# w_ada's products in pairs over quarters of PSUM, columns by transposes, and both first gate weights measured over TensorE

## The chip, the cores and the metric

The kernel runs on one core of one Trainium2 chip. The metric is the time of one execution on the device in microseconds (us), as the median of several runs. Times inside one execution come from one profiled execution, counted from the start of its span.

## What is computed

One decoder layer over 2048 tokens of width 1024, in float32. Cut to what matters here:

```
mod = silu(c) @ w_ada + b_ada            # (1, 3*1024)
shift, scale, gate = split(mod, 3)
h = rms_norm(x, g_pre) * (1 + scale) + shift
proj = h @ w_in        # qa, ka, va, fa, za, qb, kb, vb, zb
oa = forgetting_attention(qa, ka, va, fa + b_fgate) * silu(za)
ob = sliding_window_attention(rope(qb), rope(kb), vb, sinks) * silu(zb)   # window 128, 8 heads, 2 kv heads
y = concat(oa, ob) @ w_out
out = x + gate * rms_norm(y, g_post)
```

## The kernel before, in words

TensorE (PE) multiplies float16 pairs: every operand is split into a high and a low half, and a product is three matmuls (high times high, high times low, low times high). So each weight slice of `w_in` (128 columns) is loaded, its largest absolute value found (`w_max` or a reduction), turned into a power-of-two scale (`w_scale`), and split (`w_high` on ScalarE, ACT; `w_low` in two parts on VectorE, DVE). A product of a slice with one of four chunks of 512 tokens takes eight units of three matmuls.

**First stage** (a hand-written order; every engine executes its instructions in the order in which the code records them). It computes the two first thirds of `mod`: half 1 of `w_ada` (scale) and half 0 (shift), each eight tiles `wa` of 128 x 1024, loaded by the SyncE queue (SP) into eight buffers that half 0 reuses after half 1. In before, six tiles of half 1 and four of half 0 go through PE with `silb` (silu(c) spread over 128 columns) as weights, so that every one of PSUM's 128 partitions holds the same row of `mod` (L471, L589); the others are summed on DVE (L478, L480) and added by a product with ones. `ada_col` (L490, L492) turns the row into columns: times the identity, then summed along the free axis. From both halves comes a bound on h and from it a common scale `pH`, then the columns `Gp` and `Shp`. Meanwhile four x tiles are squared on ACT (`squares`, L372), normalised (`root`, `normal`), transposed on PE into `px` (`turn`, L390), and scaled by `Gp`, `Shp` on ACT into float32 `hf` and partly the float16 high half (L396); DVE makes the missing high halves (L400) and the low half (L401) of `hT[0]`. The weights `kb`, `vb` are measured over TensorE: a column of maxima is transposed, reduced, and sent to all partitions by a product with ones.

**First chunks.** For each chunk `ci` of 512 tokens the units stand in a list: kb, vb, and for `ci` < 3 the gate slices zb0 and zb1. `fill` runs through the list and before a unit runs the events hung at its number; every second unit a `tick` lets evacuations proceed, in steps that `after(n, f)` counts. The transposes of the next chunk stand between the gate units. The three PSUM banks `bk` are taken in turn and freed by the evacuation. The rotary evacuation (`evac_rope`) of kb copies the product (`qf`, ACT L697), sends it with four SP transfers to exchanged partitions (`qs`), multiplies by the cosine on DVE (`qc`, which frees the bank), by the sine on GpSimd (POOL, L711), adds (DVE L712) and splits into `stb`.

zb0's maximum is taken in the first stage (L633) and spread over PE inside the list (`z_row` at unit 6, `z_all` at 10, both in `bk[2]`, which also takes the second half of vb's product). zb1 goes another way, that of all later weights: its maxima go to DRAM (`mx_d`, POOL L214) and come back spread over the partitions (`mxr`, POOL L219), a reduction (L230) and `w_scale` follow, then `w_high` (L245) and `w_low` (L251).

**Sliding windows.** 32 windows of 256 queries (`Pair`) are interleaved with the remaining products. Each window has four ticks; DVE and ACT take the softmax, PE the scores (L831), transposes (L864) and values (L883). In passing, the squares of `w_out` are summed: 32 tiles `wsq`, loaded by SP and squared on ACT (L1085) one window later. Then follow the forgetting attention and the output product, which the change leaves alone.

Of the kernel before, what the change touches and what calls it, by code (L numbers as in the profile page):

```python
# [18 lines left out]
P = 128  # L19
# [21 lines left out]
def hybrid_layer(  # L41
# [109 lines left out]
    mxs = const.tile([P, 3], F32, name="mxs")  # L151
# [7 lines left out]
    mz = const.tile([1, 1], F32, name="mz")  # L159
# [26 lines left out]
    def after(n, f):  # L186
        late.append([n, f])
# [10 lines left out]
    first = ("kb", "vb", "zb0")  # L198
# [187 lines left out]
    def turn(ci, k):  # L386
# [6 lines left out]

        def scaled():
            for dst in ([hi] if k % 2 == 0 else []) + [hf[:]]:
                A.activation(dst, px[:], AF.Identity, scale=Gp[:, k:k + 1], bias=Shp[:, k:k + 1])  # L396

        def split():
            if k % 2:
                V.tensor_copy(hi, hf[:])  # L400
            V.tensor_tensor(lo, hf[:], hi, op=ALU.subtract)  # L401
# [19 lines left out]
    with tc.manual_schedule():  # L421
        rows = st.tile([P, P], F32, name="rows")
        posi = st.tile([P, CH], I32, name="posi")
        ifr = st.tile([P, 1], F32, name="ifr")
        V.memset(rows[:], 0.0)
# [11 lines left out]
        for k in range(1):  # L437
            load_ada(1, k)

        for g in range(4):  # L440
            SP.dma_start(posi[32 * g:32 * g + 32, :], positions[0, g * CH:(g + 1) * CH].partition_broadcast(32))
        SP.dma_start(ifr[:], inv_freq)
        for k in range(1, KT):
# [17 lines left out]
        silb = st.tile([P, KT, P], F32, name="silb")  # L461
        V.tensor_copy(silb[:], sil[:].unsqueeze(2).broadcast_to([P, KT, P]))

# [3 lines left out]
        acc = [st.tile([P, D], F32, name=f"acc{n}") for n in range(2)]  # L467

        def ada_mm(half, lhsT, rows_, begin, end):
            for n in range(2):  # L470
                PE.matmul(pm[half][n][:], lhsT, rows_[:, n * CH:(n + 1) * CH], start=begin, stop=end)  # L471

        def ada_pe(half, k, begin=False, end=False):
            ada_mm(half, silb[:, k, :], wa[half, k], begin, end)

        def ada_dve(half, k, first_):
            if first_:
                V.tensor_scalar(acc[half][:], wa[half, k][:], sil[:, k:k + 1], None, op0=ALU.mult)  # L478
            else:
                V.scalar_tensor_tensor(acc[half][:], wa[half, k][:], sil[:, k:k + 1], acc[half][:],  # L480
                                       op0=ALU.mult, op1=ALU.add)

        def ada_sum(half, end):
            ada_mm(half, ones[:], acc[half], False, end)

        def ada_col(half, dst):

            for n in range(2):
                dg = acc[half][:, n * CH:(n + 1) * CH].rearrange("p (k n) -> p k n", k=4)
                V.tensor_tensor(dg, pm[half][n][:].rearrange("p (k n) -> p k n", k=4),  # L490
                                ident[:].unsqueeze(1).broadcast_to([P, 4, P]), op=ALU.mult)
                V.tensor_reduce(dst[:, 4 * n:4 * n + 4], dg, axis=AX.X, op=ALU.add)  # L492

# [55 lines left out]
        for k in (0, 1, 3, 4, 6, 7):  # L549
            ada_pe(1, k, k == 0)  # L550
        for k in (2, 5):
            ada_dve(1, k, k == 2)
        for k in range(3):
            load_ada(0, k)
        for t in range(4):
            load_x(t)
        for k in range(3, KT):
            load_ada(0, k)
# [3 lines left out]
        ada_sum(1, True)  # L562

        mx3 = st.tile([P, 2], F32, name="mx3")
        for n, key in enumerate(first[:2]):
            V.tensor_reduce(mx3[:, n:n + 1], wq[key][0][:], axis=AX.XY, op=ALU.max, apply_absolute_value=True)
        ada_pe(0, 0, True)
        ada_pe(0, 3)
        PE.transpose(bk[0][0:2, 0:P], mx3[:], ident[:])
        ada_pe(0, 5)  # L570
        ada_dve(0, 1, True)
        ada_dve(0, 2, False)
        squares(0)
        scl0 = col8("scl0")
        ada_col(1, scl0)
        root(0)
        normal(0)
        m3 = st.tile([2, 1], F32, name="m3")
        V.tensor_reduce(m3[:], bk[0][0:2, 0:P], axis=AX.X, op=ALU.max)
        dg3 = st.tile([2, 2], F32, name="dg3")  # L580
        V.tensor_scalar(dg3[:], ident[0:2, 0:2], m3[:], None, op0=ALU.mult)
        PE.matmul(bk[0][:, P:P + 2], ones[0:2, :], dg3[:], start=True, stop=True)
        ada_dve(0, 4, False)
        ada_dve(0, 6, False)

        for n in range(2):
            nn = slice(n * CH, (n + 1) * CH)
            PE.matmul(pm[0][n][:], ones[:], acc[0][:, nn], start=False, stop=False)
            PE.matmul(pm[0][n][:], silb[:, KT - 1, :], wa[0, KT - 1][:, nn], start=False, stop=True)  # L589
        V.tensor_copy(mxs[:, 0:2], bk[0][:, P:P + 2])  # L590
        for n, key in enumerate(first[:2]):
            wq[key].append(mxs[:, n:n + 1])
        w_scale("kb")
        w_high("kb")
        w_scale("vb")
        w_low("kb", 0, 1)
        scl1 = col8("scl1")
        V.tensor_tensor(scl1[:], scl0[:], cols[:, 24:32], op=ALU.add)
        gcol = col8("gcol")
        V.scalar_tensor_tensor(gcol[:], scl1[:], 1.0, cols[:, 8:16], op0=ALU.add, op1=ALU.mult)  # L600
        absg = col8("absg")
        V.scalar_tensor_tensor(absg[:], gcol[:], -1.0, gcol[:], op0=ALU.mult, op1=ALU.max)
        turned = [turn(0, k) for k in range(5)]
        squares(1)
        w_high("vb")
        shf0 = col8("shf0")
        ada_col(0, shf0)
        shf = col8("shf")
        V.tensor_tensor(shf[:], shf0[:], cols[:, 16:24], op=ALU.add)
        abss = col8("abss")  # L610
        V.scalar_tensor_tensor(abss[:], shf[:], -1.0, shf[:], op0=ALU.mult, op1=ALU.max)
        bnd = col8("bnd")
        V.scalar_tensor_tensor(bnd[:], absg[:], 32.0, abss[:], op0=ALU.mult, op1=ALU.add)
        bmx = st.tile([P, 1], F32, name="bmx")
        V.tensor_reduce(bmx[:], bnd[:], axis=AX.X, op=ALU.max)

        PE.transpose(bk[0][0:1, 0:P], bmx[:], ident[:])
        bm = st.tile([1, 1], F32, name="bm")
        V.tensor_reduce(bm[:], bk[0][0:1, 0:P], axis=AX.X, op=ALU.max)
        PE.matmul(bk[0][:, P:P + 1], ones[0:1, :], bm[:], start=True, stop=True)  # L620
        pow2_floor(pH[:], bk[0][:, P:P + 1], "p2t")
# [3 lines left out]
        V.tensor_scalar(Shp[:], shf[:], ipH[:], 2.0 ** 14, op0=ALU.mult, op1=ALU.mult)  # L625

        V.tensor_scalar(pfl[:], ipH[:], 0.5, None, op0=ALU.mult)
        w_low("vb", 0, 1)
        for k in range(KT):
            turned[k][0]()  # L630
            turned[k][1]()
            if k == 2:
                V.tensor_reduce(mxs[:, 2:3], wq["zb0"][0][:], axis=AX.XY, op=ALU.max, apply_absolute_value=True)  # L633
            if k + 5 < KT:
                turned.append(turn(0, k + 5))
        root(1)
        normal(1)
# [48 lines left out]

    def evac_rope(ci, finish, pool):
        cols_ = slice(ci * CH, (ci + 1) * CH)

        def evac(ps, free):  # L690
# [20 lines left out]
            after(5, lambda: G.tensor_tensor(qs[:], qs[:], sinT[:, cols_], op=ALU.mult))  # L711
            after(6, lambda: V.tensor_tensor(qc[:], qc[:], qs[:], op=ALU.add))  # L712
# [886 lines left out]
```

## Time and profile before

| | |
|---|---|
| median of 3 runs | 1227.26 us (1226.62 to 1228.86) |
| profiled execution, its own time | 1225.7 us |
| its span | 1223.5 us |
| PE busy | 1161.8 us, 95% of the span |
| DVE, ACT busy | 906.5 and 674.6 us |

The 2.2 us between the profiled execution's time and its span lie outside the instructions. A timeline row gives start, duration, engine, line, operation, output and inputs, and in brackets how long the engine had been idle and what ended that. Rows with the same line and operation are merged with a count. In PE's rows a float32 matmul stands as two passes. A row that ends in an issuing queue (SPq, POOLq) is the issue of a transfer, not the transfer.

### The profile page before, as it was taken

What the parts mean: (1) busy time and instruction counts of PE and PEld (TensorE: products, weight loads), DVE (VectorE), ACT (ScalarE), POOL (GpSimd) and SP (SyncE); (2) the same over time, 40 slices, a digit from 0 to 9 for tenths busy, and PEclk for the clock granted to TensorE, in tenths of its full rate; (3) what the DMA queues carried; (4) which work ended last, traced back from release to release, by engine and by line L of the source; (5) the groups of instructions that cost most, each with busy time, mean ns of one, the idle gap of its engine ahead of it and who ended that gap; (6) DMA issues with size and microseconds to landing.
All of it is one profiled execution on the core that took longest, in us unless ns stands there. A gap on an engine that the chain in (4) does not pass through costs nothing.

```text
span 1223.5 us, 27396 instructions
## 1 busy us (share of the span) xinstructions
PE 1161.8 (95%) x10832; PEld 694.4 (57%) x10832; DVE 906.5 (74%) x2268; ACT 674.6 (55%) x1117; POOL 141.4 (12%) x252
## 2 busy tenths in 40 slices
PE   6769999999999999999999999999999979999997
PEld 2446746755558985555555555555555546555553
DVE  6756656677877656788888799878978797676665
ACT  2665434555555461466666666666766788433231
POOL 2001122233323210101000110010000000000000
PEclk8879999999999999999999999999999999999999
DMA  9654432423423432223325322122111146446652
GB/s 322 204 123 130 115 76 64 69 77 94 90 64 89 65 56 57 73 57 92 66 75 73 92 66 71 42 64 55 41 40 45 45 130 190 134 158 195 191 172 84
DMA packets 88036, 120.71 MB, mean 99 GB/s; under 512 B 27836, under 2 KB 63716, under 8 KB 87908
## 3 DMA queue, kind: packets, MB, share of 16 engines
q1 hardware_dynamic: 76932, 85.94, 24.9%
q0 software_dynamic: 10976, 33.03, 11.7%
q8 instruction: 85, 1.39, 0.6%
q14 instruction: 43, 0.35, 0.1%
HBM read 71.56 MB, written 25.18 MB: 79 GB/s over the span
## 4 chain that ended last, share of the span: by engine, by line
PE 79%; DVE 9%; DMA 4%; issue 3%; SPq 2%; ACT 2%; POOL 1%; DVEq 0%; POOLq 0%; ACTq 0%
PE bk L307 31%; PE bk L1407 13%; PE bk L325 6%; PE sta L1258 4%; PE bk L1209 4%; PE sta L1259 4%; PE poa L1284 2%; PE poa L1285 2%; PE poa L1282 2%; PE pxb L864 2%; PE pss L831 2%; PE pob L883 2%; DVE pha L1272 2%; DVE a_m L1212 1%; PE bk L1370 1%
## 5 line engine op out<-in xcount | busy, mean ns | idle before, releaser
L1265 ACT ACTIVATE p<-sta,lift,scl_qk 128x1024 f32<-128x1024 f32 (+2 forms) x160 | 171.8, 1074 | 134.3 <-PE sta L1259 78.5
L307 PE MATMUL bk<-hT,wh_qk 128*128 128x512 f16 x768 | 194.7, 379 | 0.4 <-DVE a_m L1212 0.4
L1407 PE MATMUL bk<-wohl,oz 128*128 128x512 f16 x768 | 172.4, 379 | 1.8 <-ACT wohl L1347 0.8
L1272 DVE TENSOR_TENSOR pha<-p,pha 128x1024 f16<-128x1024 f32 (+2 forms) x160 | 169.2, 1057 | 0.0
L1212 DVE TENSOR_REDUCE a_m<-bk 128x1 f32<-128x512 f32 x192 | 130.3, 686 | 52.3 <-PE bk L1209 51.7
L1269 ACT ACTIVATE pha<-p 128x1024 f16<-128x1024 f32 (+2 forms) x160 | 148.0, 925 | 7.3 <-PE poa L1285 1.4
L1407 PEld LDWEIGHTS <-oz 128*128 128x128 f16 x768 | 74.4, 99 | 83.8 <-issue 1.8
L1282 PE MATMUL poa<-vt,pha 128*128 128x65 f16 x1088 | 116.9, 193 | 3.0 <-DVE ona L1291 3.0
L1285 PE MATMUL poa<-vt,pha 128*128 128x65 f16 x1088 | 116.7, 193 | 1.1 <-DVE pha L1272 1.1
L1284 PE MATMUL poa<-vt,pha 128*128 128x64 f16 x1088 | 117.0, 195 | 0.0
L1258 PE MATMUL sta<-T 128*128 128x512 f16 (+1 forms) x320 | 112.0, 350 | 4.7 <-ACT p L1265 4.6
L307 PEld LDWEIGHTS <-wh_qk 128*128 128x128 f16 x768 | 72.4, 97 | 75.2 <-issue 1.4
L1209 PE MATMUL bk<-T 66*128 66x512 f16 (+2 forms) x320 | 109.9, 350 | 2.8 <-DMA T<-stq 2.3
L1282 PEld LDWEIGHTS <-pha 128*128 128x128 f16 x1088 | 101.9, 97 | 17.8 <-DVE ona L1291 4.3
L1259 PE MATMUL sta<-T 69*128 69x512 f16 (+1 forms) x320 | 110.7, 351 | 0.0
L1284 PEld LDWEIGHTS <-pha 128*128 128x128 f16 x1088 | 101.2, 97 | 11.5 <-issue 0.3
L1285 PEld LDWEIGHTS <-pha 128*128 128x128 f16 x1088 | 101.2, 99 | 1.3 <-DVE pha L1272 1.3
L307 PE MATMUL bk<-hT,wh_zb 128*128 128x512 f16 x384 | 92.4, 386 | 9.8 <-ACT wh_zb L245 9.1
L307 PE MATMUL bk<-hT,wh_za 128*128 128x512 f16 x384 | 99.9, 379 | 0.0
L325 PE MATMUL bk<-wh_va,hT 128*128 128x128 f16 x1536 | 91.2, 220 | 0.0
L325 PEld LDWEIGHTS <-hT 128*128 128x128 f16 x1536 | 87.5, 98 | 5.4 <-issue 2.6
L307 PE MATMUL bk<-hT,wh_qb 128*128 128x512 f16 x384 | 87.4, 380 | 0.0
(491 smaller groups left out, 1880.1 us busy)
## 6 DMA issues: line engine op xcount, KB each, us to landing
wa<-in_w_ada_dram SPq DMA_DIRECT2D x16, 512.0 KB
z_d<-tz POOLq DMA_DIRECT2D x32, 256.0 KB, 2.9
T<-stq SPq DMA_DIRECT2D x128, 64.0 KB
T<-o_d SPq DMA_DIRECT2D x16, 512.0 KB
T<-z_d SPq DMA_DIRECT2D x16, 512.0 KB
xr<-in_x_dram SPq DMA_DIRECT2D x16, 512.0 KB
out_dram<-yg SPq DMA_DIRECT2D x15, 512.0 KB
xt<-in_x_dram SPq DMA_DIRECT2D x12, 512.0 KB
```

The lines of the kernel that those rows point to most:

```text
L307: PE.matmul(ps, whl[:, a, k, :], hT[ci][:, b, k, :], start=(k == 0 and n == 0), stop=(k == KT - 1 and n == 2))
L325: PE.matmul(ps[:, u * P:(u + 1) * P], hT[ci][:, a, k, u * P:(u + 1) * P], whl[:, b, k, :], start=(k == 0 and n == 0), stop=(k == KT - 1 an ...
L1209: PE.matmul(mx[:, :w], T[0:XM, 0, i * P:(i + 1) * P], T[0:XM, 2, pc * CH:pc * CH + w], start=True, stop=True)
L1258: PE.matmul(self.st[:, o:o + w], T[:, 3, kb_], T[:, 1, qc], start=True, stop=False)
L1259: PE.matmul(self.st[:, o:o + w], T[0:XR, 2, kb_], T[0:XR, 0, qc], start=False, stop=not diag)
L1265: A.activation(self.p32[:, :self.w], self.st[:, :self.w], AF.Exp, scale=scl[f"qk{self.hd}"][:], bias=lift[:])
L1269: A.activation(self.ph[:, 0, :self.w], self.p32[:, :self.w], AF.Copy)
L1272: V.tensor_tensor(self.ph[:, 1, :self.w], self.p32[:, :self.w], self.ph[:, 0, :self.w], op=ALU.subtract)
L1282: PE.matmul(po[:, u, :], ph[:, 0, pq], vt[:, b, hd, 0:65], start=(self.first and n == 0 and u == 0), stop=False)
L1284: PE.matmul(po[:, u, 0:64], ph[:, 0, pq], vt[:, b, hd, 65:VW], start=False, stop=False)
L1285: PE.matmul(po[:, u, :], ph[:, 1, pq], vt[:, b, hd, 0:65], start=False, stop=(self.last and n == len(self.blocks) - 1))
L1407: PE.matmul(py, self.hl[:, i, k, :], w_slot(8 * j + k)[:, cc], start=(k == 0 and m_ == 0), stop=(k == KT - 1 and m_ == 2))
```

## The change

- All sixteen tiles of `w_ada` go through PE, two at a time: `silb` has only 32 columns per tile, and tile k writes into quarter k mod 4 of PSUM's partitions (k and k+4 add up). Each half is then copied to SBUF (`ada_row`, ACT), transposed in 128-column blocks (`ada_turn`, PE), and the four quarters are summed by a reduction of 16 values per row (`ada_col`).
- The bound that leads to `pH` is taken apart: the part from half 1 and the biases (`pre`) is ready early; half 0 gives only the largest absolute value of its rows (`rm`, `rmx`), added over the quarters by a product with `sel`.
- `inv_freq` and the positions are loaded from ACT's queue; `zb0` is no longer loaded a second time by POOL; x tiles 0 to 3 are loaded before half 0; zb1 is loaded by SP in the first stage.
- zb0 and zb1 are both measured over PE (`z_row` at 8, `z_all` at 11). zb1's scale and split stand at units 18 to 25 of the list.
- For chunk 0, ACT makes the high half of tiles 0 and 4 only. `squares(1)` follows the whole of chunk 0's scaling; `root(1)` and `normal(1)` move into the list; the transposes of chunk 1 stand three units later.
- In the sliding windows the rotary evacuation's later steps come one tick later, and `wsq` has three buffers and is squared two windows after its load instead of one.

```diff
-    first = ("kb", "vb", "zb0")
+    first = ("kb", "vb", "zb0", "zb1")
...
+        high = k % 2 == 0 if ci else k in (0, 4)
...
+        A.dma_start(ifr[:], inv_freq)
+        for g in range(4):
+            A.dma_start(posi[32 * g:32 * g + 32, :], positions[0, g * CH:(g + 1) * CH].partition_broadcast(32))
...
-        for key in first:
+        for key in first[:2]:
             w_load(key, pieces(key))
...
-        silb = st.tile([P, KT, P], F32, name="silb")
+        silb = st.tile([P, KT, 32], F32, name="silb")
...
+        def ada_two(half, k):
             for n in range(2):
+                for k_ in (k, k + 1):
+                    q = slice(32 * (k_ % 4), 32 * (k_ % 4) + 32)
+                    PE.matmul(pm[half][n][q, :], silb[:, k_, :], wa[half, k_][:, n * CH:(n + 1) * CH],
+                              start=k_ < 4, stop=k_ >= 4)
+        def ada_row(half, n):
+            A.activation(arow[half][:, n * CH:(n + 1) * CH], pm[half][n][:], AF.Copy)
+        def ada_turn(half, n):
+            for k in range(4):
+                PE.transpose(pm[half][n][:, k * P:(k + 1) * P], arow[half][:, (4 * n + k) * P:(4 * n + k + 1) * P],
+                             ident[:])
+        def ada_col(half, n, dst):
+            V.tensor_reduce(dst[:, 4 * n:4 * n + 4],
+                            pm[half][n][:].rearrange("p (k q r) -> p k q r", k=4, q=4)[:, :, :, 0],
+                            axis=AX.X, op=ALU.add)
...
         for t in range(4):
             load_x(t)
-        for k in range(3, KT):
+        for k in range(KT):
             load_ada(0, k)
         w_load("zb0", pieces("zb0"), SP)
         for t in range(4, 8):
             load_x(t)
-        ada_sum(1, True)
+        w_load("zb1", pieces("zb1"), SP)
+        for k in range(0, KT, 2):
+            ada_two(1, k)
...
+        for k in range(0, KT, 2):
+            ada_two(0, k)
+        rm = st.tile([P, 2], F32, name="rm")
+        for n in range(2):
+            V.tensor_reduce(rm[:, n:n + 1], pm[0][n][:], axis=AX.X, op=ALU.max, apply_absolute_value=True)
+            ada_row(0, n)
...
+        turned = [turn(0, 0)]
+        ada_turn(0, 0)
+        turned.append(turn(0, 1))
+        PE.matmul(bk[0][:, P:P + 1], sel[:], rmx[:], start=True, stop=True)
+        ada_turn(0, 1)
+        turned += [turn(0, k) for k in (2, 3, 4)]
...
-        root(1)
-        normal(1)
+        V.tensor_reduce(mxs[:, 3:4], wq["zb1"][0][:], axis=AX.XY, op=ALU.max, apply_absolute_value=True)
+        squares(1)
...
-    at_slice(6, z_row)
-    at_slice(10, z_all)
+    at_slice(8, z_row)
+    at_slice(11, z_all)
+    at_slice(9, lambda: root(1))
+    for u in range(4):
+        at_slice(10 + u, lambda u=u: normal(1, (u,)))
...
+            d = turn_lag[0]
+            after(5 + d, lambda: G.tensor_tensor(qs[:], qs[:], sinT[:, cols_], op=ALU.mult))
...
-        wsp = swa_pool("wsp", 2)
+        wsp = swa_pool("wsp", 3)
```

How the order moves is shown at three places. The first is PE at half 0 of `w_ada`; before, `wa` tiles with 128 columns of weights, and sums of ones with `acc`, the part summed on DVE:

```order
L471 MATMUL bk_135<-wa_281,silb 128x512
L471 MATMUL bk_136<-wa_281,silb 128x512
L582 MATMUL bk_134<-dg_349,ones 128x2
L588 MATMUL bk_135<-acc_202,ones 128x512
L589 MATMUL bk_135<-wa_285,silb 128x512
L588 MATMUL bk_136<-acc_202,ones 128x512
L589 MATMUL bk_136<-wa_285,silb 128x512
L390 MATMUL px<-ident,xt_269 128x128
```

The same place on PE in the change, from the last pair of tiles on; 32x512 is the output, `bk_134` and `bk_135` are the two banks of half 0:

```order
L474 MATMUL bk_134<-wa_272,silb 32x512
L474 MATMUL bk_134<-wa_274,silb 32x512
L474 MATMUL bk_135<-wa_272,silb 32x512
L474 MATMUL bk_135<-wa_274,silb 32x512
L389 MATMUL px<-ident,xt_252 128x128
L389 MATMUL px<-ident,xt_254 128x128
L389 MATMUL px<-ident,xt_256 128x128
L389 MATMUL px<-ident,xt_258 128x128
L482 MATMUL bk_134<-ident,arow_205 128x128 x4
```

No matmul waits for a sum made on DVE any more; the transposes of x and of the row take the place of the sums. The second place is DVE behind chunk 0, in before: `w_mx` is zb1's reduction, whose way goes over DRAM, and `mxr` what comes back; `stb` is kb's rotary result.

```order
L752 SCALAR_TENSOR_TENSOR vb<-bk_136,vb 128x2x64 x2
L754 SCALAR_TENSOR_TENSOR fl<-bk_136,kf,bfg 128x16
L230 TENSOR_REDUCE w_mx_767<-mxr 128x1
L86 TENSOR_SCALAR w_p_770<-w_mx_767 128x1
L87 TENSOR_SCALAR w_pw<-w_p_770 128x1
L236 RECIPROCAL w_sw<-w_pw 128x1
L237 TENSOR_SCALAR w_sw<-w_sw 128x1
L706 TENSOR_TENSOR stb<-qc,stb 128x512
```

There, in the change, up to the point where the measured maxima leave PSUM (`bk_135`):

```order
L106 SCALAR_TENSOR_TENSOR rst<-rs_t,rs_y 128x4
L699 SCALAR_TENSOR_TENSOR qc<-bk_133,cosT 128x512
L383 TENSOR_SCALAR hT_107<-hT_107,rst 128x1024
L937 COPY mxs<-bk_135 128x2
L383 TENSOR_SCALAR hT_107<-hT_107,rst 128x1024
L86 TENSOR_SCALAR w_p_685<-mxs 128x1
```

The copy of the maxima now stands behind the root of chunk 1, the cosine product and one normalisation; the reduction over `mxr` is gone for zb1. The third place is ACT after chunk 0, in the change; `wh_zb_798` is zb1's high half, `tz` a gate's tanh, `junk` a square of an x tile of chunk 2:

```order
L711 ACTIVATE stb<-qc 128x512
L397 ACTIVATE hT_105<-px,Shp,Gp 128x512
L397 ACTIVATE hf<-px,Shp,Gp 128x512
L244 ACTIVATE wh_zb_798<-wr_zb_282,w_sw 128x1024
L397 ACTIVATE hf<-px,Shp,Gp 128x512
L397 ACTIVATE hT_105<-px,Shp,Gp 128x512
L397 ACTIVATE hf<-px,Shp,Gp 128x512
L350 ACT_TABLE_LOAD
L350 ACTIVATE tz<-bk_133,cz_zb_766 128x512
L397 ACTIVATE hf<-px,Shp,Gp 128x512
L371 ACTIVATE junk,ss<-xt_699 128x1024
```

All of chunk 1's scaling now stands behind `stb`, that is behind the whole rotary evacuation of chunk 0's kb; before, its first tile stood ahead of it.

More of the change, by code (lines that the diff above doesn't have):

```diff
@@ L466, in hybrid_layer @@
         pm = {1: [ps_x.tile([P, CH], F32, tag="x", name="pm") for _ in range(2)], 0: [bk[1], bk[2]]}
[L467 to L469 removed]
+        arow = [st.tile([P, D], F32, name=f"arow{n}") for n in range(2)]
+        def ada_two(half, k):
             for n in range(2):
[L471 to L474 removed]
@@ L596, in hybrid_layer @@
+        normal(0)
         w_low("kb", 0, 1)
[L597 to L606, printed above, removed]
```

164 lines of the change are left out of this document (76 added, 88 removed).

## The prediction

> **What bounds the kernel now.** I read the waits of PE first, since PE is busy 1161.8 of 1223.5 us, the busiest engine; columns: engine and line, who ended the wait, total, times, longest.
>
> ```profile
> PE bk L307 <- ACT wh_zb L245: 9.1, 1, 9.1
> PE bk L307 <- ACT hT L396: 3.5, 1, 3.5
> PE pob L883 <- DVE ptb L869: 3.0, 2, 2.1
> PE pss L831 <- issue: 1.6, 1, 1.6
> ```
>
> The longest wait of all is one for zb1's high half. The busy times by stretch say where PE idles: columns are the stretch, its length, then busy time of PE, PEld, DVE, ACT, POOL, granted clock, DMA share, GB/s.
>
> ```profile
> 0.00:83.00 83.00, 54.14 (x256) 29.32 (x256) 54.48 (x142) 39.24 (x59) 10.41 (x21) 0.87 0.74 230
> 83.00:150.00 67.00, 66.29 (x510) 42.99 (x510) 41.86 (x102) 39.72 (x67) 8.80 (x12) 0.96 0.44 120
> 150.00:260.00 110.00, 105.08 (x1089) 69.51 (x1086) 69.63 (x209) 51.03 (x139) 27.28 (x49) 0.98 0.32 68
> ```
>
> 29 us are idle before 83 us, 0.7 in the next 67, 4.9 in the 110 after. From 83 us on PE sets the pace, so what is won before is kept. I therefore follow the first 98 us to one mark, the end of kb's product of chunk 1, and treat the windows apart. The timeline's rows on the way to it:
>
> ```profile
> 32.49 1.98 PE L471 MATMUL bk<-wa,silb 128*128 128x512 f32 x4 [2.63 <-DMA wa<-in_w_ada_dram]
> 35.05 1.99 PE L471 MATMUL bk<-wa,silb 128*128 128x512 f32 x4 [0.47 <-DMA wa<-in_w_ada_dram]
> 40.46 1.02 PE L589 MATMUL bk<-wa,silb 128*128 128x512 f32 x2
> 46.97 1.06 ACT L372 ACTIVATE junk<-hT 128x1024 bf16<-128x1024 f32 x1 [1.86 <-DMA hT<-in_x_dram]
> 49.93 0.59 PE L307 MATMUL bk<-hT,wh_kb 128*128 128x512 f16 x1 [3.50 <-ACT hT L396]
> 57.77 1.73 PE L307 MATMUL bk<-hT,wh_kb 128*128 128x512 f16 x6
> 65.87 0.81 PE L307 MATMUL bk<-hT,wh_zb 128*128 128x512 f16 x3
> 73.69 0.54 POOL L219 DMA_DIRECT2D mxr<-mx_d  x1 [7.85 <-DMA cosT<-cs__241]
> 79.80 0.29 DVE L230 TENSOR_REDUCE w_mx<-mxr 128x1 f32<-128x128 f32 x1 [2.41 <-DMA mxr<-mx_d]
> 82.08 1.03 PE L307 MATMUL bk<-hT,wh_zb 128*128 128x512 f16 x2 [9.12 <-ACT wh_zb L245]
> 92.39 5.34 PE L307 MATMUL bk<-hT,wh_kb 128*128 128x512 f16 x24
> ```
>
> Transfers bind until half 0 of w_ada has landed, then a chain over PE, DVE and ACT leads to the first kb product at 49.93; kb ends at 59.5 and zb0 starts at 65.87. zb1's way over DRAM (back at 79.80) holds PE until 82.08. The mark is at 97.7 (92.39 + 5.34).
>
> **Step 1, the last tile of w_ada lands.** Tiles 3 and 5 of half 0 end waits at 32.49 and 35.05: 1.28 us per tile, so tile 7 lands near 37.6. The bytes ahead of it stay the same, less POOL's extra load of zb0 (1024 x 128 numbers, a tile's size, so 1.28 us). The positions leave SP's queue, which should let the first tiles follow closer; I give that 0.8 us, between 0 and 3. Forecast 35.5 (33.5 to 36.3).
>
> **Step 2, its products.** Four matmuls follow its landing, eight passes. In a steady run each pass has one weight load like this:
>
> ```profile
> 27.98 0.19 PEld L471 LDWEIGHTS bk<-wa,silb 128*128 128x128 f32 x1 [0.24 <-issue]
> ```
>
> So a pass starts every 0.19 + 0.24 = 0.43 us. One after the other the eight take 3.44 us, fully overlapped in pairs 1.72. No run shows a matmul on a quarter of the columns; these are the two ends. I take 1.72, since neighbours in the order write different quarters: 37.2. The Trainium skill's page "TensorE: Matmul & The Clock Gate", Part 3, gives 2.38 times for three column tiles; by that, as an estimate 1.59 times for two, the eight would take 2.16 us and the sum be 0.4 us worse.
>
> **Step 3, from the last product to kb.** Before, 41.5 (40.46 + 1.02) to 49.93: 8.45 us, with masked sums on DVE, then ACT held by `squares(1)`, which waited for x until 46.97, and by wh_vb. Both leave this place. What is left, priced by these rows of the groups (mean ns behind the comma):
>
> ```profile
> L492 DVE TENSOR_REDUCE shf<-acc 128x4 f32<-128x512 f32 x2 | 1.4, 686 | 0.1
> L396 ACT ACTIVATE hf<-px,Shp,Gp 128x512 f32<-128x512 f32 x20 | 15.1, 780 | 0.3 <-PE px L390 0.3
> L401 DVE TENSOR_TENSOR hT<-hf,hT 128x512 f16<-128x512 f32 x20 | 13.3, 688 | 1.8 <-ACT hf L396 1.5
> L400 DVE CAST hT<-hf 128x512 f16<-128x512 f32 x10 | 4.2, 423 | 3.3 <-ACT hf L396 3.3
> L633 DVE TENSOR_REDUCE mxs<-wr_zb 128x1 f32<-128x1024 f32 x1 | 1.2, 1212 | 0.0
> L104 DVE TENSOR_TENSOR rs_t<-rs_t,rs_v 128x4 f32<-128x4 f32 x9 | 1.5, 162 | 0.3
> ```
>
> One reduction of a bank after the last product (0.7, the other overlaps), 0.3 of crossing, `rmx` 0.2; then sel's two passes, under 0.43 each, behind transposes of x and of the row, with the crossing to DVE 1.4; seven small DVE operations at 0.2 (0.16 and a gap) are 1.5; ACT's first scaling 0.8 and 0.1 to PE. Sum 5.0 (4 to 6). kb starts at 42.2, 7.7 us early.
>
> **Step 4, kb of chunk 0.** DVE binds: after the first `hf` (0.75) come 8 x 0.69 + 6 x 0.42 + 1.21 = 9.3, plus gaps 0.4; before, four casts only, 0.85 less. kb ends at 52.9 against 59.5: 6.6 early.
>
> **Step 5, to zb0.** The prices, beside the small operations above:
>
> ```profile
> L372 ACT ACTIVATE junk<-xt 128x1024 bf16<-128x1024 f32 x8 | 8.4, 1054 | 3.8 <-DMA xt<-in_x_dram 3.5
> L372 ACT ACTIVATION_READ_ACCUMULATOR junk<-xt 128x1 f32 x8 | 1.5, 189 | 0.0
> 61.16 3.72 PE L740 MATMUL bk<-wh_vb,hT 128*128 128x136 f16 x60
> ```
>
> The new waits: `z_row` on PE needs zb1's maximum, queued on DVE behind the whole loop, so all of vb's product stands 0.9 us, until 53.9. `squares(1)`, four times 1.25 on ACT behind the last scaling at 48.2, ends at 53.3. On DVE zb1's maximum and five small operations last to 54.9, the root of 13 operations at 0.17 to 57.2, then cosine and one normalisation, 0.7 each, and only then are the maxima copied out of `bk[2]` at 58.7. PE's second half of vb (48 matmuls at 0.062, 3.0 us) needs that bank; the first is done at 57.2 with the small products between: another 1.7 us idle. zb0's scale on DVE (a normalisation and four small operations later) is ready at 60.3, its high half on ACT at 61.4, hidden by vb, which ends at 62.0. zb0 starts at 62.1: only 3.8 us early.
>
> **Step 6, zb0 and zb1.** A tile's transposes and two units, in chunk 1:
>
> ```profile
> 104.33 0.60 PE L390 MATMUL px<-ident,xt 128*128 128x128 f32 x4
> 104.77 1.46 PE L307 MATMUL bk<-hT,wh_zb 128*128 128x512 f16 x6
> 106.07 0.60 PE L390 MATMUL px<-ident,xt 128*128 128x128 f32 x4
> ```
>
> From start to start 0.44 and 1.30 (0.22 a matmul): 48 matmuls are 10.4, eight tiles of transposes 3.5, together 13.9. The wait for DRAM is gone. What is late next is kb's rotary result, then zb1's high half:
>
> ```profile
> 103.50 1.27 POOL L711 TENSOR_TENSOR qs<-qs,sinT 128x512 f32<-128x512 f32 x1 [7.80 <-DMA qs<-qf]
> 98.43 3.53 SPq L699 DMA_DIRECT2D qs<-qf  x4
> L245 ACT ACTIVATE wh_zb<-wr_zb,w_sw 128x1024 f16<-128x1024 f32 x2 | 2.3, 1146 | 2.0 <-DVE w_sw L237 2.0
> 84.05 1.28 ACT L351 ACT_TABLE_LOAD   x1
> ```
>
> In chunk 1 the exchange takes 5.1 us from issue to POOL's multiply. From `qf` at 53.9 that gives 59.3; POOL is free by then. DVE's add stands behind zb0's low half (62.9), so `stb` runs on ACT at 64.1. Then two scalings, 66.2, and zb1's high half until 67.4. PE needs it at 69.0. zb1 hides; kb of chunk 1 may start at 76.0.
>
> **Step 7, kb of chunk 1.** From `stb` on, ACT has no gap: 12 scalings x 0.77, zb1's half 1.15, the table load 1.28, two tanh and `stb` at no more than a scaling, 2.1, four squares 5.0: 18.7 from 64.1, so the last `hf` ends at 82.7. Cast and subtraction on DVE, 1.2, and one unit, 0.65: the mark at 84.6. PE alone would reach it at 81.3, so ACT costs 3.3. Gain 97.7 - 84.6 = **13.1**. Chunks 1 and 2 stay PE's: ACT needs some 18 of 24.7 us there.
>
> **Step 8, the windows.** Between 150 and 260 us:
>
> ```profile
> DVE qc L712 <- POOL qs L711: 15.0, 5, 8.1
> ACT wsq L1085 <- DMA wsq<-in_w_out_dram: 5.5, 1, 5.5
> 215.56 0.69 DVE L706 TENSOR_TENSOR stb<-qc,stb 128x512 f16<-128x512 f32 x1
> 217.36 0.83 PE L831 MATMUL pss<-kst,stb 64*128 64x256 f16 x12
> 225.80 0.72 PE L831 MATMUL pss<-kst,stb 64*128 64x256 f16 x10
> ```
>
> The tick and the third buffer shorten waits by which DVE and ACT hand `ptb` late to PE (3.0). POOL's share, waiting for maxima from DRAM, stays. I take half, 1.5; bounds: all 4.6 with the issue gap, or 2.1 lost (one tick, a quarter of the window from 217.36 to 225.80). At the end two squares instead of one: 0.6 on ACT, partly seen, I take 0.3.
>
> **The sum.** 13.1 + 1.5 - 0.3 = 14.3. The profiled execution's 1225.7 (span 1223.5 and 2.2 around it) becomes 1211.4. It lies 1.6 under the median of 1227.26; the same saving gives **1213.0**.
>
> **The rivals.** First, the pairs don't overlap (20%). Half 0 is then 32 passes of 0.43, 13.8 us, started when its second tile is there (35.5 - 6 x 1.28 = 27.8): 41.6, not 37.2. All behind comes 4.4 later: 1217.4. For it: float32 passes that each fill the array's time; against: different quarters. The same page and Part 3 say that weight loads overlap running matmuls only when the row group differs, and here all 128 rows are used by both; by that rule this case happens, and no run here shows it.
>
> Second, faster (8%): the copy of step 5 and ACT's queue of step 7 cost nothing, because the early transfers run at full rate and the squares end sooner. 1.7 + 3.3 come back: 1208.0.
>
> Third, slower (6%): the later rotary steps reach the scores. A piece's `stb` is done at 215.56, its scores start at 225.80: 10.2 us slack, 9.5 beyond the row's own duration. A tick is 2.1. Only if POOL's and DVE's waits grow by over 7 us besides does each of the 14 pieces cost a tick: 29 less the gain of 13.1 and 0.3 more at the end, about 1243. Waits of 8.1 are in the table; but these are paid already.
>
> Fourth, no change (4%): a stall at zb0 or at kb of chunk 1 takes all 13.1 back, as when x of chunk 2 lands over 10 us after its square is due (72 us): 1227. Before, those loads were never waited for.
>
> **How the numbers follow.** The forecast has 62%. Its own range: step 1 (-2, +0.8), step 3 (1 either way), step 8 (-3, +3.7), rarely together: 1208 to 1217. With the first rival at the upper end and the second at the lower: 1207 to 1220. A measurement can tell about 0.2%, 2.5 us. Faster: 62 + 20 + 8 = 90%; same 4%; slower 6%.
>
> **What would show it.** Right: PE's nine-us wait for wh_zb gone; half 0's last product 1.7 to 2 us after its transfer; kb first at 41 to 43.5; idle of 1 to 2 us ahead of vb's second half, ended by the copy of the maxima; the mark at 83 to 86, waiting for ACT's `hf`. Wrong: pairs 0.86 apart or more per matmul; kb after 45; a wait over 3 us at zb1; POOL or DVE waits in the windows that stop PE's scores.

## The result, and the profile of the changed kernel

The changed kernel takes 1232.18 us (median of 20 runs, 1227.34 to 1237.46); the kernel before, on the same chip, 1224.91 us (20 runs). The ratio is 1.0059, 95% interval 1.0045 to 1.0073: slower by 0.6%, where 1.2% faster was forecast. The profiled execution took 1233.82 us, its span 1232.1 us.

First PE's busy time by stretch in the changed kernel; the first three rows are the stretches that the prediction showed of before, the last is the stage of the forgetting attention, from its first product on PE (426.24 us) to the end of the span.

```profile
0.00:83.00 83.00, 64.67 (x394) 32.69 (x395) 57.82 (x176) 51.07 (x78) 9.10 (x19) 0.98 0.70 236
83.00:150.00 67.00, 67.00 (x524) 42.83 (x522) 40.81 (x108) 34.40 (x60) 9.50 (x12) 1.00 0.46 119
150.00:260.00 110.00, 109.58 (x1177) 71.71 (x1175) 79.55 (x228) 59.21 (x165) 32.18 (x61) 1.00 0.36 80
...
426.24:1232.11 805.87, 757.47 (x6680) 420.62 (x6676) 604.03 (x1426) 440.01 (x570) 40.20 (x64) 0.98 0.34 88
```

The same stage in the kernel before, where it begins at 449.49:

```profile
449.49:1223.52 774.03, 748.40 (x6680) 417.71 (x6676) 603.54 (x1426) 439.78 (x568) 40.18 (x64) 0.99 0.34 91
```

Up to 260 us the changed kernel is the better one: 18.3 us idle instead of 28.9 before 83 us, none in the next stretch, 0.4 instead of 4.9 in the third. It reaches the forgetting attention 23.3 us earlier. Then it loses: 31.8 us more for a stage whose instructions the change does not touch. With the same number of matmul records (6680) PE is idle 48.4 us there instead of 25.6, and busy 9.1 us longer. The timeline on the way to the mark, in the changed kernel:

```profile
35.94 1.90 PE L474 MATMUL bk<-wa,silb 128*32 128x512 f32 x6 [0.30 <-DMA wa<-in_w_ada_dram]
...
41.70 0.38 PE L306 MATMUL bk<-hT,wh_kb 128*128 128x512 f16 x1 [0.29 <-ACT hT L397]
...
52.41 0.27 PE L931 MATMUL bk<-ident,mxs 128*2 128x128 f32 x1 [0.54 <-DVE mxs L631]
...
57.11 3.00 PE L738 MATMUL bk<-wh_vb,hT 128*128 128x136 f16 x48 [1.18 <-DVE mxs L937]
59.95 1.47 PE L306 MATMUL bk<-hT,wh_zb 128*128 128x512 f16 x6
...
73.82 4.94 PE L306 MATMUL bk<-hT,wh_kb 128*128 128x512 f16 x21
...
79.87 0.59 PE L306 MATMUL bk<-hT,wh_kb 128*128 128x512 f16 x2 [0.35 <-DVE hT L402]
```

The mark is at 80.5 (79.87 + 0.59), 17.2 us before the old one; 13.1 was forecast. From kb's start on everything ahead of it came as forecast or sooner; the last tile of `w_ada` came 0.4 us later than forecast. The waits of PE in the changed kernel show where it went afterwards:

```profile
PE bk L1218 <- DMA T<-rw: 10.5, 1, 10.5
PE poa L1293 <- issue: 8.9, 2, 6.2
...
PE sta L1268 <- issue: 3.8, 1, 3.8
```

The wait for `wh_zb` is gone. In its place stand 10.5 us for a transfer of rows into T (L1182), in the forgetting attention, and stops that the trace puts down to no semaphore. The rows of the timeline where PE goes on, in the changed kernel:

```profile
453.90 0.26 PE L1218 MATMUL bk<-T 66*128 66x128 f16 x1 [10.52 <-DMA T<-rw]
...
579.90 0.21 PE L1293 MATMUL poa<-vt,pha 128*128 128x64 f16 x1 [6.18 <-issue]
580.92 0.21 PE L1294 MATMUL poa<-vt,pha 128*128 128x65 f16 x1 [0.81 <-issue]
...
722.26 0.49 PE L1268 MATMUL sta<-T 69*128 69x384 f16 x1 [3.83 <-issue]
...
863.30 0.19 PE L1293 MATMUL poa<-vt,pha 128*128 128x64 f16 x1 [2.77 <-issue]
```

Around each of them PE's clock is halved for a while. Busy times in the four stretches of half clock (granted clock is the third column from the right), changed kernel:

```profile
448.20:458.40 10.20, 4.50 (x13) 1.78 (x14) 1.48 (x6) 0.60 (x1) 0.54 (x1) 0.50 0.42 10
577.90:584.70 6.80, 3.99 (x11) 1.41 (x11) 1.80 (x3) 1.19 (x2) 1.07 (x2) 0.50 0.44 76
721.30:728.10 6.80, 5.84 (x24) 2.48 (x25) 5.51 (x10) 3.15 (x4) 1.07 (x2) 0.50 0.60 94
864.70:868.10 3.40, 3.40 (x23) 1.75 (x22) 3.19 (x12) 2.26 (x3) 0.00 (x0) 0.50 0.78 133
```

17.7 us of PE's busy time were at half clock there; if the same work takes half as long at full clock, 8.9 us were lost (an estimate). The first row shows something else: the DMA engines moved 10 GB/s in it. The Trainium skill's page "TensorE: Matmul & The Clock Gate", Part 1, says that the clock halves after an idle window of some 3.4 us; the first row agrees, at 0.50 from 4.8 us into 10.5 us of waiting on. The fourth stands behind a stop of 2.77 us, which is shorter than that.

What these stops have in common is found on POOL. Ahead of four of the eight heads, the maxima of a qk weight and of a za weight go to DRAM back to back (`mx_d`, L213) and are read back spread over the partitions (`mxr`, L218). POOL's timeline at the first of these pairs, changed kernel:

```profile
437.71 0.58 POOL L213 DMA_DIRECT2D mx_d<-w_mx  x1 [9.84 <-DVE w_mx L210]
438.83 0.55 POOL L213 DMA_DIRECT2D mx_d<-w_mx  x1 [0.54 <-DVE w_mx L210]
446.55 0.54 POOL L218 DMA_DIRECT2D mxr<-mx_d  x1 [7.17 <-DMA mx_d<-w_mx]
455.88 0.54 POOL L218 DMA_DIRECT2D mxr<-mx_d  x1 [8.79 <-DMA mx_d<-w_mx]
```

The same pair in the kernel before:

```profile
460.57 0.58 POOL L214 DMA_DIRECT2D mx_d<-w_mx  x1 [9.45 <-DVE w_mx L211]
461.69 0.55 POOL L214 DMA_DIRECT2D mx_d<-w_mx  x1 [0.54 <-DVE w_mx L211]
469.10 1.19 POOL L219 DMA_DIRECT2D mxr<-mx_d  x2 [6.86 <-DMA mx_d<-w_mx]
```

Both issue the two writes 1.1 us apart. Before, both are done some 8 us later and the reads follow each other; now the second write is done 9.3 us after the first. At the four pairs the reads stand 0.7, 1.8, 1.3 and 1.6 us apart before, and 9.3, 11.0, 9.4 and 9.3 in the changed kernel. PE's stops lie inside these four.

Between the two reads of a pair the core's transfers nearly stand. The columns as above, for the first two pairs in the changed kernel (3 and 4 GB/s; at the other two 17 and 5):

```profile
446.60:455.80 9.20, 1.90 (x6) 0.83 (x7) 0.47 (x3) 0.00 (x0) 0.49 (x1) 0.59 0.32 3
570.80:581.70 10.90, 3.59 (x39) 1.99 (x37) 4.01 (x10) 1.49 (x3) 0.50 (x1) 0.83 0.27 4
```

### The profile page after: what moved, and what is told of

It is laid out like the page before. It is cut to its first block, busy times and chain, and to the rows that moved or that the text cites. A ratio compares the mean times of both kernels' runs of the same rounds, so it can differ in the third digit from the quotient of the medians.

```text
span 1232.1 us, 27468 instructions
## 1 busy us (share of the span) xinstructions
PE 1163.2 (94%) x10866; PEld 689.5 (56%) x10866; DVE 899.2 (73%) x2273; ACT 674.8 (55%) x1119; POOL 138.7 (11%) x248
## 4 chain that ended last, share of the span: by engine, by line
PE 78%; DVE 8%; DMA 6%; issue 4%; ACT 3%; SPq 1%; POOL 0%; DVEq 0%; ACTq 0%; POOLq 0%
PE bk L306 29%; PE bk L1416 13%; PE bk L324 7%; PE bk L1218 4%; PE sta L1267 4%; PE sta L1268 4%; PE poa L1293 2%; PE poa L1291 2%; PE poa L1294 2%; PE pxb L862 2%; PE pss L829 2%; DMA wa<-in_w_ada_dram 2%; PE pob L881 2%; DMA T<-rw 1%; DVE pha L1281 1%
## 5 line engine op out<-in xcount | busy, mean ns | idle before, releaser
L1218 PE MATMUL bk<-T 66*128 66x512 f16 (+2 forms) x320 | 111.1, 354 | 11.0 <-DMA T<-rw 10.5
L1293 PEld LDWEIGHTS <-pha 128*128 128x128 f16 x1088 | 101.7, 98 | 14.3 <-issue 3.3
L306 PE MATMUL bk<-hT,wh_za 128*128 128x512 f16 x384 | 103.6, 390 | 0.0
L306 PE MATMUL bk<-hT,wh_zb 128*128 128x512 f16 x384 | 89.8, 379 | 0.0
L1223 DVE CUSTOM_DVE_ANT_0 bk<-bk,cmask 128x128 f32<-128x128 f32 (+3 forms) x128 | 63.1, 493 | 35.1 <-PE bk L1218 34.5
```

Of the source, the lines that this page charges most:

```text
L306: PE.matmul(ps, whl[:, a, k, :], hT[ci][:, b, k, :], start=(k == 0 and n == 0), stop=(k == KT - 1 and n == 2))
L1218: PE.matmul(mx[:, :w], T[0:XM, 0, i * P:(i + 1) * P], T[0:XM, 2, pc * CH:pc * CH + w], start=True, stop=True)
L1293: PE.matmul(po[:, u, 0:64], ph[:, 0, pq], vt[:, b, hd, 65:VW], start=False, stop=False)
```

## The experiments

Theory S (slots, the numbers of the rows) at first, A (their addresses) later: the place of the `mx_d` rows decides. Rivals: T, the late stages are reached 25 us earlier and collide with their own transfers; W, an edit in the windows. The change takes zb1 off the way over DRAM, so every later weight moves by one in the rotation of three rows. Before, the pairs took rows 0 and 1, now they take 2 and 0.

### Other row numbers (e1, e2, e3)

```diff
-        md = mx_d[len(kaps_seen) % 3]
+        md = mx_d[(len(kaps_seen) + 1) % 3]     # e1; + 2 in e2, and + 2 in the kernel before (e3)
```

> The changed kernel with one number added to the index of the three DRAM rows mx_d, so that the two maxima that are written back to back before each head (qk's and za's) go to rows 0 and 1, as before the change, instead of rows 2 and 0. Nothing else moves. Theory S (slots): the second of two neighbouring writes lands 9 to 11 us late only because its row is no longer next to the first one's; then the two reads back (mxr) stand 0.5 to 2 us apart again, the wait of 10.5 us for T<-rw and the gaps of 6.2, 3.8 and 2.8 us go, the half-clock stretches behind them (10.2, 6.8, 6.8, 3.4 us) go with them, and the 25 us that were won by the end of the windows are kept: 1200 us (1195 to 1206). Theory T (time): the stalls come from reaching the forgetting attention 25 us earlier than its transfers allow, whatever rows are written: 1232 us (1227 to 1237), the wait for T<-rw at 10 us. Theory W (windows): the third buffer, the lag or the squares in the windows are to blame: 1232 us as well.

> The changed kernel with the pairs in rows 1 and 2: neighbours, but not the first two. Theory S in its plain form (neighbours land together): as with rows 0 and 1, 1200 us (1195 to 1206). Theory S in the form that only a pair within the first 1024 bytes lands together: second landing 9 to 11 us late, 1232 us. Theories T and W: 1232 us (1227 to 1237).

> The kernel before the change with the pairs moved to rows 2 and 0 (the index counts from 2): nothing of the change itself is in it. Theory S: the second landing of each pair comes 9 to 11 us late here too, with PE waits of 3 to 10 us and half-clock stretches in the forgetting attention: 1245 us (1232 to 1262). Theories T and W: no change, 1225 us (1222 to 1229).

e1: 1229.58 us, ratio 1.0032 (1.0012 to 1.0051); e2: 1229.74, 1.0034 (1.0015 to 1.0053); e3: 1224.23, 0.9999 (0.9982 to 1.0015). Nothing moved, the reads of a pair stood 8.6 to 11.0 us apart in e1 and e2, 0.7 to 2.8 in e3. By the numbers of the rows, theory S fell. But the three kernels had tested nothing: the built programs give DRAM areas their addresses in the order of first use, so the names were exchanged and every write kept its address. Before: 81920 for the first row used, ahead of `z_d`, because zb1's maximum is written before the first gate product; the next two lie behind `z_d`, at 8474624 and 8478720. In the changed kernel all three lie behind `z_d`, at 8470528, 8474624, 8478720, and the pair is the third and the first: 8192 bytes apart instead of 8.4 MB.

### No DRAM for the maxima (e4)

```diff
-        G.dma_start(md[:], mx[:])
-        wq[key].append(md)
+        wq[key].append(mx)
...
-        G.dma_start(mxr[:], wq[key].pop().rearrange("p o -> (p o)").partition_broadcast(P))
-        wq[key].append(mxr)
+        row = bk[bank()][0:1, 0:P]
+        PE.transpose(row, wq[key].pop()[:], ident[:])
+        mone = sm(1, "w_m1")
+        V.tensor_reduce(mone[0:1, :], row, axis=AX.X, op=ALU.max)
+        wq[key].append(mone)
...
-            V.tensor_reduce(mx2[:], mxr[:], axis=AX.X, op=ALU.max)
+            mx2 = bk[bank()][:, 0:1]
+            PE.matmul(mx2, ones[0:1, :], mxr[0:1, :], start=True, stop=True)
```

> The changed kernel with no DRAM write or read for the later weights' maxima: each is turned by one transpose on TensorE (0.27 us in the first stage's rows), reduced on VectorE, and given to all partitions by a product with ones (0.19 us a pass, two passes), 22 times: 22 x 0.5 = 11 us more of TensorE, while VectorE has 0.2 us less in each reduction. Theory S: the long landings are gone with the writes, so 1200 + 11 = 1211 us (1202 to 1218), and no transfer of the late stage lands over 5 us late. Theories T and W: the stalls stay, 1232 + 11 = 1243 us (1235 to 1250).

1209.41 us, ratio 0.9878 (0.9856 to 0.9900). The stops are gone with the writes, and T and W with them: the same windows and the same early arrival, and no late transfer. PE pays for it in this group of e4:

```profile
L215 PE MATMUL bk<-ident,w_mx 128*1 128x128 f32 x22 | 5.7, 272 | 0.4 <-DVE a_m L1220 0.4
```

### The distance of the pair (f1 to f4, g1, g2, h2)

```diff
-    mx_d = [dram.tile([P, 1], F32, name=f"mx_d{n}") for n in range(3)]
+    mx_d = [dram.tile([8200, P, 1], F32, name=f"mx_d{n}") for n in range(3)]   # f1, first row of each
+    mx_d = dram.tile([3, P, 1], F32, name="mx_d")                             # f3
...
-        md = mx_d[len(kaps_seen) % 3]
+        md = mx_d[len(kaps_seen) % 2]                                         # f2
+        md = mx_d[1 + len(kaps_seen) % 2 if kaps_seen else 0]                 # f4, kernel before
```

g1 and g2 are like f1, with areas of 4096 and 8192 bytes (g1) or 8192 and 8192 (g2) ahead of the third row; h2 is f4 with areas of 8192 bytes.

> The changed kernel with each of the three DRAM rows mx_d at the head of an area of its own of 4.2 MB, so that the pair of rows that is written back to back lies 8.4 MB apart (before the change: 8.4 MB; in the changed kernel and in both kernels that renumbered its rows: 8192 bytes, since rows are given addresses in the order of their first use, and the renumbering changed no address). Instructions, waits and their order are the same. Theory A (addresses): two such writes wait for one another only when their rows lie close; then the reads back of a pair stand 0.5 to 3 us apart, the 10-us wait for T<-rw and the gaps of 3 to 6 us go, and the time is 1200 us (1194 to 1207). Theory T (time: the late stages are reached 25 us earlier than their transfers allow) and theory W (the edits in the windows): 1231 us (1226 to 1237).

> The changed kernel with two rows used in turn instead of three, so that the pair lies 4096 bytes apart. Theory A with closeness as such: late second landings as at 8192 bytes, 1231 us (1226 to 1237). Theory A with one address bit that sends rows to different places: at 4096 bytes the bit differs, and the pairs land together, 1200 us (1194 to 1207). Theories T and W: 1231 us.

> The changed kernel with the three rows side by side in one DRAM area, the pair 1024 bytes apart. Theory A in either form: late second landings, 1231 us (1226 to 1237), or worse by up to 3 us if nearer rows cost more. Theories T and W: 1231 us. It bounds what closeness can cost.

> The kernel before the change with its first row used once (for zb1) and the other two in turn, so that the pairs lie 4096 bytes apart instead of 8.4 MB; nothing of the change is in it. Theory A with closeness as such: the reads back of a pair 9 to 11 us apart here too, PE waits of 3 to 10 us at three or four heads and half-clock stretches behind them, 1250 us (1235 to 1262). Theory A with one address bit: 1225 us. Theories T and W: no change, 1225 us (1221 to 1229).

> The changed kernel with the pair of rows 12288 bytes apart (three times 4096). Theory A as it stands after six kernels (late where the pair's distance is an even multiple of 4096 bytes: 8192 and 8.4 MB; on time at 1024, 4096 and 8.4 MB plus 4096): reads back of each pair 0 to 3 us apart, 1202 us (1199 to 1206). If only nearness to the same or the neighbouring page counts: late by 9 to 11 us, 1231 us (1226 to 1237).

> The changed kernel with the pair 16384 bytes apart (four times 4096). Theory A by even multiples: second landings late by 9 to 11 us at all four pairs, the wait for T<-rw at 10 us, 1231 us (1226 to 1237). If 8192 is special: on time, 1202 us (1199 to 1206).

> The kernel before the change with the pairs 8192 bytes apart, and nothing of the change in it. If an even multiple of 4096 bytes is what costs, it costs here too: second landings 15 to 19 us after their issue, a wait of some 8 to 11 us for T<-rw, gaps of 3 to 7 us in the forgetting attention, and with f4 (1222) as the base 22 to 34 us more: 1250 us (1240 to 1258). If it takes the changed kernel's earlier arrival as well (theory T in part): 1225 us (1220 to 1232).

The last column but one is the time from the first product of `const_rows`, where the forgetting attention's stage begins on PE, to the end of the span; g1 and g2 have one timed run each, so no interval.

| kernel | pair apart, bytes | reads apart, us | stage to end, us | median, us | ratio to before (95%) |
|---|---|---|---|---|---|
| before | 2049 x 4096 | 0.7 to 1.8 | 774.0 | 1224.91 | |
| changed | 2 x 4096 | 9.3 to 11.0 | 805.9 | 1232.18 | 1.0059 (1.0045 to 1.0073) |
| f1, changed | 2050 x 4096 | 9.1 to 11.5 | 807.3 | 1231.18 | 1.0058 (1.0039 to 1.0076) |
| f2, changed | 4096 | 0.6 to 1.4 | 775.2 | 1201.91 | 0.9808 (0.9785 to 0.9831) |
| f3, changed | 1024 | 0.5 to 1.7 | 775.1 | 1202.04 | 0.9807 (0.9783 to 0.9831) |
| f4, before | 4096 | 1.1 to 2.1 | 776.9 | 1222.14 | 0.9980 (0.9963 to 0.9998) |
| g1, changed | 3 x 4096 | 0.9 to 1.3 | 775.6 | 1203.40 | |
| g2, changed | 4 x 4096 | 7.9 to 10.3 | 799.6 | 1227.33 | |
| h2, before | 2 x 4096 | 7.7 to 10.9 | 798.3 | 1247.41 | 1.0182 (1.0157 to 1.0207) |

f1 went against theory A as it stood, that near rows are what costs: with 8.4 MB between them the pair was as late as with 8192 bytes. f2, 4096 bytes apart, was on time. So was f3, 1024 bytes apart, against both forms of theory A that were put down for it. What sorts all nine rows is whether the distance is an even multiple of 4096 bytes (in f3 both rows lie in one block of 4096 bytes). g1 and g2 were forecast from that and came out so. h2 puts the bad distance into the kernel before, with nothing of the change in it: 1247.41 against f4's 1222.14, 25.3 us. So the earlier arrival plays no part that the cost needs. POOL's timeline of f2 at the first pair, to be read against the changed kernel's above:

```profile
436.66 0.58 POOL L213 DMA_DIRECT2D mx_d<-w_mx  x1 [9.84 <-DVE w_mx L210]
437.78 0.55 POOL L213 DMA_DIRECT2D mx_d<-w_mx  x1 [0.53 <-DVE w_mx L210]
444.63 1.12 POOL L218 DMA_DIRECT2D mxr<-mx_d  x2 [6.30 <-DMA mx_d<-w_mx]
```

And f2's stage of the forgetting attention, then its first two pairs from the first read on, as long as the changed kernel's two rows:

```profile
425.19:1200.42 775.23, 749.34 (x6680) 418.49 (x6676) 603.77 (x1426) 440.52 (x570) 40.19 (x64) 0.99 0.34 91
...
444.60:454.00 9.40, 9.39 (x58) 4.80 (x59) 6.70 (x22) 1.46 (x3) 1.08 (x2) 1.00 0.36 65
559.70:570.00 10.30, 9.97 (x111) 5.88 (x110) 8.26 (x17) 5.37 (x7) 1.57 (x3) 1.00 0.58 117
```

Full clock, PE busy, and transfers at 65 and 117 GB/s (131 and 72 at the other two pairs). f2 waits 2.3 us for T at the place where the changed kernel waits 10.5. The balance against f2: 10.5 - 2.3 at T, 6.2 + 0.8 + 3.8 + 2.8 in the stops and 8.9 by the clock are 30.7 us; the stage is 30.6 us longer (805.87 - 775.23), 22.5 of it idle time of PE and 8.1 busy time. f2 and f3 are the fastest of all versions; e4, g1, g3, g4 and h1 beat both kernels as well.

### The old addresses in the changed kernel (h1)

```diff
         V.tensor_copy(mxs[:, 2:4], bk[2][:, P:P + 2])
+        G.dma_start(mx_d[2][:], mxs[:, 2:3])
```

> The changed kernel with one more 512-byte write (zb0's maximum into row 2, never read) ahead of the first z_d store, as zb1's trip through DRAM did before the change. Row 2 thereby lies ahead of z_d, and the pairs have the very addresses that they had before: 81920 and 8474624. If the moved rows are all that the removed trip cost: reads back 0 to 3 us apart, 1202 us (1199 to 1207), with up to 2 us for the added write. If anything else of the change reaches the late stages: above 1210 us.

1205.52 us, ratio 0.9842 (0.9826 to 0.9859); reads 0.6 to 1.4 us apart, stage to end 776.0. One more write, which nobody reads, saves some 27 us, because it moves the addresses of the pair (and with them those of the third row and of `z_d`). Nothing else of the change costs the late stages more than some 2 us (776.0 against 774.0 in before). h1 is 3.6 us slower than f2 by the medians, but the intervals overlap, so a price of the added write is not shown.

### The pairs of products, and the windows (g3, g4)

Both start from f2.

```diff
-                    q = slice(32 * (k_ % 4), 32 * (k_ % 4) + 32)
+                    q = slice(32 * (k // 2), 32 * (k // 2) + 32)     # g3, start and stop within the pair
...
-        turn_lag[0] = 1                                               # g4, with two wsq buffers again
```

> The changed kernel with the pair of rows 4096 bytes apart (ratio to before 0.981) and with the two products of each pair in the same quarter of PSUM's partitions, so that they can't lie over one another. If the pairs overlapped (steps of the prediction), the last pair of w_ada's first half costs 3.4 us instead of 1.7, and the mark and the end move by 1.7 us to 3.5 us: ratio 0.9825 to 0.984. If they never overlapped (the prediction's first rival), nothing moves: ratio 0.981.

> The changed kernel with the pair of rows 4096 bytes apart and the edits in the windows undone (lag 0, two wsq buffers, square of the tile before). As the prediction sized them (a gain of 1.5 us, bounds -2.1 to 4.6): 1201.9 + 1.5 = 1203.4 us, ratio 0.982. If they carry what was won between the mark (17 us) and the end of the windows (25 us): 1201.9 + 8 = 1210 us, ratio 0.988, and the waits for ptb and stb are back in the windows.

g3: 1203.78 us, ratio 0.9827 (0.9804 to 0.9850), not told apart from f2 by the time. The trace tells it. The last passes of half 0 in f2, with a pair in two quarters, as PE's matmuls and then their weight loads:

```profile
35.84 1.90 PE L474 MATMUL bk<-wa,silb 128*32 128x512 f32 x6 [0.38 <-DMA wa<-in_w_ada_dram]
...
35.84 0.14 PEld L474 LDWEIGHTS bk<-wa,silb 128*32 128x32 f32 x4 [1.29 <-DMA wa<-in_w_ada_dram]
36.30 0.11 PEld L474 LDWEIGHTS bk<-wa,silb 128*32 128x32 f32 x1 [0.31 <-issue]
36.72 0.11 PEld L474 LDWEIGHTS bk<-wa,silb 128*32 128x32 f32 x1 [0.32 <-issue]
```

All of half 0 in g3, with a pair in one quarter, and its last weight loads:

```profile
28.97 11.32 PE L474 MATMUL bk<-wa,silb 128*32 128x512 f32 x32
...
38.42 0.11 PEld L474 LDWEIGHTS bk<-wa,silb 128*32 128x32 f32 x1 [0.32 <-issue]
38.85 0.11 PEld L474 LDWEIGHTS bk<-wa,silb 128*32 128x32 f32 x1 [0.32 <-issue]
39.28 0.11 PEld L474 LDWEIGHTS bk<-wa,silb 128*32 128x32 f32 x1 [0.32 <-issue]
```

In f2 four loads fall into 0.14 us, and six passes are done in four steps of 0.43: the first two start together, so do the next two, and the last two stand alone. In g3 the last passes start one by one, 0.43 apart. So products in different quarters do overlap, and those in one quarter do not. g3 takes the overlap away only inside a pair: it still gets through 32 passes in 11.3 us, where 32 times 0.43 are 13.8, because a pair also lies over its neighbours in other quarters. PE works through half 0 without a pause there, until 40.3, and ends at 37.7 in f2, where it waits for tiles. kb starts 2.4 us later in g3 (43.98 against 41.61); these 2.4 us are not the price of the overlap alone, as PE also ran at half clock until 34 us in g3 and until 31.3 in f2.

g4: 1205.75 us, ratio 0.9836 (0.9815 to 0.9857), against 0.9808: the window edits are worth some 3.4 us by the ratios. The intervals overlap, but the forgetting attention's stage starts at 429.5 in g4 and at 424.7 to 427.2 in the ten kernels with the edits and DRAM rows. The waits that return in g4's windows:

```profile
163.65 0.72 PE L862 MATMUL pxb<-ident,sm__1954 128*128 128x128 f32 x2 [1.16 <-ACT sm__1954 L853]
...
214.81 0.82 PE L881 MATMUL pob<-vb,ptb 128*128 128x64 f16 x22 [1.00 <-DVE ptb L867]
```

## Why the prediction was wrong

Steps 1 to 6 and 8 held or came close, and step 7 put a cost too high. What failed is the premise ahead of them, "From 83 us on PE sets the pace, so what is won before is kept". The busy table of before allowed it as far as 260 us, and I carried it to the end. The stages behind have transfers just ahead of PE, and the change altered one thing about them that no order of instructions shows: where three DRAM rows lie. zb1's way over DRAM was costed as a wait that goes ("The wait for DRAM is gone"); that its write also put the first row ahead of `z_d` was not seen. The sum had no term for the late stage; the runs showed one of 30.6 us against f2: PE's stops and its half clock around the four late pairs. With the pairs' distance mended (f2), the change gains 1.9%, 1224.3 to 1201.9. These 22.4 us are also more than the 14.3 of the sum, and f2 lies below its range: the mark gave 17.2 instead of 13.1, the windows 3.4 instead of 1.5, and some 2 us are not assigned.

- **Step 1**: the last tile ended PE's wait at 35.94, forecast 35.5. **Step 2**: its products took 1.90, forecast 1.72. That the two lie so near is luck in part: six passes follow the landing, not eight, since the first of the four matmuls needs only the tile before, and not all of them overlap, as g3's comparison shows. Eight passes in full overlap would be four steps of 0.43, and so are the six. By the Trainium skill's page "TensorE: Matmul & The Clock Gate", Part 3, weight loads overlap with running matmuls only when the row group differs; read so, the first rival would have happened. The measurement speaks against it for outputs in different column quarters: f2's four loads in 0.14 us run on into passes that use the same 128 rows.
- **Step 3**: kb started at 41.70, forecast 42.2. 3.9 us instead of 5.0: slightly below its bound of 4. **Step 4**: kb ended at 51.9, forecast 52.9.
- **Step 5**: the waits were 0.54 and 1.18, forecast 0.9 and 1.7; zb0 started at 59.95, forecast 62.1. **Step 6**: 13.87 from there to kb, forecast 13.9.
- **Step 7** was mis-sized. ACT's chain still came last, but it cost PE two waits of 0.39 and 0.35 us, not 3.3. ACT in the changed kernel:

```profile
62.08 0.63 ACT L711 ACTIVATE stb<-qc 128x512 f16<-128x512 f32 x1 [1.49 <-DVE qc L710]
62.62 0.76 ACT L397 ACTIVATE hT<-px,Shp,Gp 128x512 f16<-128x512 f32 x1
63.28 0.77 ACT L397 ACTIVATE hf<-px,Shp,Gp 128x512 f32<-128x512 f32 x1
...
77.85 0.78 ACT L397 ACTIVATE hf<-px,Shp,Gp 128x512 f32<-128x512 f32 x1
```

  `stb` came at 62.1, not 64.1, and the chain behind it took 16.6 us, not 18.7: a scaling lasts 0.77, but the next starts after 0.66. Durations summed in a row count that overlap double.
- **Step 8**: the window edits gave 3.4, forecast 1.5, inside its bounds. Between the mark (17.2 us) and the start of the forgetting attention (426.24 against 449.49: 23.3) lie 6 us; the rest of them is within what before's windows vary by (that stage starts at 443.2 to 449.5 in the four kernels built from before).
- **The rivals**: the third, which ended slower, had another mechanism (late rotary steps), and no trace shows it: PE does not wait there. The second happened in part: the copy cost 1.18 us and ACT's chain 0.7. The fourth, at zb0 or kb of chunk 1, did not happen. The true one was not among them.

What stays open: why PE stops without a semaphore inside a late pair. The transfers crawl there, and if instructions, which the profile shows as a DMA queue of their own (`instruction`), are held up with them, that would do it. The trace does not show it: in the stop that ends at 579.90 no packet of that queue starts or ends (one lasts from 566.2 to 569.3, the next starts at 588.0), and no run isolates it. The rule of the even multiple was fitted to the kernels up to f4; g1, g2, h1 and h2 were forecast from it. It rests on seven distances (1024 bytes, and 1, 2, 3, 4, 2049 and 2050 times 4096). What in the memory makes it was not tried.

## What to carry to other kernels

When a change adds or removes a DRAM buffer or moves its first use, compare the addresses in the built programs, not only the order of instructions: a transfer can get slower without being touched. And where a gain is won early, follow it through the stages behind it at matched instructions before counting it as kept; here the trace shows 23 us in hand at 426 us and 9 us lost at the end.

## What the runs showed of the hardware

- A write of 128 numbers of 4 bytes to DRAM takes some 8 us until it counts as done, in every kernel here that has the pairs (7.6 to 9.4 from the first write of a pair to its read). The Trainium skill's page "DMA: Bandwidth & Descriptors", section "Anatomy of one DMA", gives a fixed cost of about 2 us per transfer; the measurement is four times that.
- Two such writes 1.1 us apart are done side by side when their rows lie in one block of 4096 bytes or an odd number of blocks apart (1, 3, 2049), and the second only after 15 to 19 us, as if one came after the other, when an even number apart (2, 4, 2050).
- While the second is late, the core's other transfers stand nearly still: 3 to 17 GB/s between the two reads at the four pairs, 65 to 131 in f2 after the first read.
- A stop of PE costs more than itself: 24.1 us of stops in late pairs brought 27.2 us at half clock with them, by estimate 8.9 us more.
- Float32 products with 32 columns of weights overlap when they write different quarters of PSUM's partitions (two passes start together, f2), and stand 0.43 us apart in one quarter (g3).
